# Weight sums of layer two's P pairs: made in the third block and kept for the fourth

## The chip, the cores and the metric

The kernel runs on one core of one Trainium2 chip. The metric is the device time of one launch in microseconds (us). Before the change three runs took 1447.68, 1449.65 and 1452.13 us; the median is 1449.65 us. The profile is of one further execution, which took 1452.83 us.

## The reference, cut to what matters

The model is two layers over 2048 tokens of width 1024. Each layer normalises, scales and shifts its input, multiplies it by `w_in` (1024 x 3072), mixes, gates, and multiplies by `w_out`:

```python
for l in range(DEPTH):                       # 2
    mod = c_act @ w_ada[l] + b_ada[l]
    shift, scale, gate = jnp.split(mod, 3, axis=-1)
    h = rms_norm(x, g_pre[l]) * (1.0 + scale[:, None, :]) + shift[:, None, :]
    proj = h @ w_in[l]                       # u_a, b_a, c_a, gate_a, u_p, gate_p: 512 columns each
    y_a = b_a * causal_depthwise_conv(c_a * u_a, w_conv[l]) * jax.nn.silu(gate_a)
    y_p = causal_multiscale_pool(u_p, w_pool[l], pool_scale[l]) * jax.nn.silu(gate_p)
    y = jnp.concatenate([y_a, y_p], axis=-1) @ w_out[l]
    x = x + gate[:, None, :] * rms_norm(y, g_post[l])
```

All of it is in float32.

## The kernel before, in words

The tokens are cut into two halves of 1024. Layer and half give four blocks: first (0,0), second (0,1), third (1,0), fourth (1,1), in this order. A block is an in-projection, with the mixing behind it, and then an out-projection; the out-projection also prepares the next block's input `h`.

A float32 matmul is made of three: every operand is split into a rounded high part (a cast on ScalarE, ACT in the profile) and a remainder (a subtraction on VectorE, DVE), and high x high, high x remainder and remainder x high are summed. So each weight tile goes through a load, a cast (line 211, or 777) and a subtraction (line 221, or 787) before TensorE (PE) may use it.

There are two forms of in-projection. The plain one (`in_phase`) takes one group of 128 output columns at a time, 8 k steps of 6 matmuls of 128x512. The other (`in_seven`) takes two groups as a pair, with the seven products of a Strassen scheme instead of eight; a product is 12 matmuls. The pairs are called P (`up` with `gp`), A (`ua` with `ca`) and B (`ba` with `ga`), four of each, i = 0 to 3. The seven products need the weight quarters A11, A12 and A22 and the four sums S1 to S4 of quarters. The first block is plain throughout; the second is plain for i = 0 and 1 and in pairs for i = 2 and 3; the third and fourth are in pairs.

Where the sums come from is what the change touches. In the second block's pairs they are made on the spot: four quarters are loaded by SyncE (SP), `add` makes the sums on VectorE (lines 758 to 760 and 765), and casts and remainders follow as for any weight. Layer two's sums are needed twice, in the third block and in the fourth; they are made ahead, as background tasks, with high part and remainder, and stored to a DRAM tensor `sums`, from which GpSimd (POOL) loads them at line 740 straight into their place. The tasks for the A and B pairs run in the first block. Those for the P pairs, `sum_task`, two for each pair, run in the second block's plain part. One of them takes two landing places, four loads (line 456), seven VectorE instructions (lines 464 to 467, 474, 476), three casts and four stores by POOL (lines 478 to 481).

The same plain part has other background tasks. First come 16 fills, which load parts of `h` (line 1123), and 8 mix tasks, which load a weight tile, multiply it on TensorE (line 421) and store it. Then come 16 finish tasks for the first block's output, with the sum tasks between them: a finish task loads two tiles (lines 1180 and 1181), multiplies and adds on VectorE (lines 1184 and 1186), stores the new residual by POOL (line 1191), and adds its square up (lines 1197 and 1200). Fills, mixes, finish and sum tasks all land in one pool `l`, five places of 128x512, and each place is free again when the last reader, a store by POOL in many cases, is done with it.

The order of the work is written out by the program: engines take their instructions in exactly the order in which the code issues them, so an instruction that waits holds up all behind it on its engine or queue. `Paced` spreads the tasks: each of 72 steps (of 96; tasks are taken from step 14 on) gets an equal share of the tasks' written costs, E2 = 0.7 us per VectorE instruction. Weights of the plain part are loaded up to five half groups ahead and their remainders made three ahead, counting the one in work; a half group is 24 matmuls. In the pairs, loads go out 6 products ahead, casts 4 and remainders 3 (`LOAD, HIGH, SETTLE`); the products' weights lie in a ring of seven places.

`working(t, r, l, w, v)` sets the numbers of places: t for wide scratch tiles, r for 128x512 scratch halves, l for landing tiles, w for raw weights, v for a partial sum.

Of the kernel before, what the change touches and what calls it, by code (L numbers as in the profile page):

```python
# [12 lines left out]
P = 128  # L13
# [9 lines left out]
NCG = 4  # L23
# [10 lines left out]
def trunk(ctx: ExitStack, tc: tile.TileContext, xt, c, wada, vec, rcp, win, wupt, wpool, wout, out):  # L34
    nc = tc.nc
# [4 lines left out]
    @contextmanager  # L40
    def working(t, r, n, w, v):

        with ExitStack() as st:
            for name, bufs in (("t", t), ("r", r), ("l", n), ("w", w), ("v", v)):
                if bufs:
                    held[name] = st.enter_context(tc.tile_pool(name=name + str(t), bufs=bufs, reuse_waits="tile"))
            yield
# [38 lines left out]
    for l in range(DEPTH):  # L86
# [10 lines left out]
    sums = {  # L97
        (l, n): dram.tile([P, 2, 4, KH * P], F32R, name=f"sums{l}_{n}") for l in range(DEPTH) for n in range(3 * NCG)
    }
# [9 lines left out]
    class Work:  # L109
# [5 lines left out]
        def __init__(self):  # L115
            self.q = []
# [314 lines left out]
    PAIRS = [(kind, i) for i in range(NCG) for kind in ("P", "A", "B")]  # L431
# [269 lines left out]
    def in_weights(l, order, first, places):  # L701
        return Weights([w_src(l, *order[n], h) for n in range(first, len(order)) for h in range(2)], places)

    PRODUCTS = (
        ("A11", "B11"), ("S2", "T2"), ("S3", "T3"), ("S1", "T1"), ("A12", "B21"), ("A22", "T4"), ("S4", "B22"),
    )
# [3 lines left out]
    SUM = {"S1": 0, "S2": 1, "S3": 2, "S4": 3}  # L710
    LOAD, HIGH, SETTLE = 6, 4, 3

    class Sevenths:


        def __init__(self, l, ring, pairs, made=False):
            self.l, self.ring, self.pairs, self.made = l, ring, pairs, made
            self.ops, self.raws = {}, {}
            self.nm = 7 * len(pairs)
            self.loaded = self.highs = self.settled = 0  # L720
# [11 lines left out]
        def load(self, upto):  # L732
            while self.loaded < min(upto, self.nm):
                m = self.loaded
                n, q = divmod(m, 7)
                a = PRODUCTS[q][0]
                if a in SUM and not self.made:
                    kind, i = self.pairs[n]
                    t = self.place(m)
                    nc.gpsimd.dma_start(t.rearrange("p a b c -> p a (b c)"), sums[self.l, PAIRS.index((kind, i))][:, :, SUM[a]])  # L740
                elif not self.made:
                    self.raws[m] = self.quarter(n, *QUARTER[a])
                elif q == 0:
                    self.raws[m] = self.raws[m + 1] = self.quarter(n, 0, 0)
                    self.raws[m + 2] = self.quarter(n, 1, 0)
                    self.raws[m + 5] = self.quarter(n, 1, 1)
                elif q == 4:
                    self.raws[m] = self.raws[m + 2] = self.quarter(n, 0, 1)
                self.loaded += 1
# [19 lines left out]
        def high(self, upto):  # L769
            self.load(upto)  # L770
            us = 0
            while self.highs < min(upto, self.nm):
                m = self.highs
                if m in self.raws:
                    if self.made:
                        us += self.add(m)
                    nc.scalar.copy(self.place(m)[:, 0], self.raws[m].rearrange("p (a b) -> p a b", b=P))  # L777
                self.highs += 1
            return us

        def low(self, upto):
            us = 0
            while self.settled < min(upto, self.nm):
                m = self.settled
                if m in self.raws:
                    t, raw = self.ops[m], self.raws.pop(m).rearrange("p (a b) -> p a b", b=P)
                    nc.vector.tensor_tensor(t[:, 1], raw, t[:, 0].bitcast(F32), op=ALU.subtract)  # L787
                    us += E2
                self.settled += 1
            return us  # L790

        def settle(self, upto):
            return self.high(upto) + self.low(upto)
# [730 lines left out]

        return ws, closing, done

    with working(5, 6, 5, 6, 2), tc.manual_schedule():
        plain = [(kind, i) for kind, i in IN_ORDER if i < PLAIN]
        pairs = [(kind, i) for kind, i in PAIRS if i >= PLAIN]
        first = in_weights(0, plain, 0, turned(ws.places, 16))  # L1530
        h, fills, opening, hrhs = out_phase(0, 0, y, 0, 1, ws, hplaces, yorder, first, True)
        ring = first.places + hplaces[8 : 8 + KH]
        wts = Sevenths(0, ring, pairs, True)
        later = Later()
        mixes = [mix_task(1, g, n, later) for g in range(NCG) for n in range(2)]
        fins = finish_tasks(0, 0, later)
        sums_ = [sum_task(1, n, u, False) for n, u in mine("P")]
        tasks = between(fills, mixes) + between(fins, sums_)
        in_phase(0, 1, hrhs, tasks, later, None, None, first.places, wts, first, opening, plain)
        hp = {}  # L1540
        for k in range(KH):
            hp["B11", k], hp["B21", k], hp["B22", k] = hplaces[k], hplaces[KH + k], hplaces[12 + k]
        it = iter(yorder)
        for name in ("T2", "T3", "T1", "T4"):
            for k in range(KH):
                hp[name, k] = next(it)
        ws, closing, done = block_end(0, 1, hp, ring, pairs, False, (3, 2, 3, 2, 2, 2))
        kept = in_seven(0, 1, h, [], None, [], later, wts, closing, pairs)
        y, yorder, wplaces, hplaces, _ = done(kept)
    with working(5, 8, 6, 3, 2), tc.manual_schedule():  # L1550
        for n, (l, b) in enumerate(blocks[2:], 2):
            lplaces = yorder[4:]
            ring = wplaces[1:] + yorder[:4] + wplaces[:1]
            wts = Sevenths(l, ring, PAIRS)
            h, fills, opening, _ = out_phase(*blocks[n - 1], y, l, b, ws, hplaces, lplaces, wts)
            hp = {}
            it = iter(hplaces)
            for k in range(KH):
                for name in ("B11", "T1", "T3", "T2"):
                    hp[name, k] = next(it)  # L1560
            it = iter(lplaces)
            for name in LATE:
                for k in range(KH):
                    hp[name, k] = next(it)
            later = Later()
            tasks = finish_tasks(*blocks[n - 1], later)
            if (l, b) == (1, 0):
                tasks = between(tasks, [ada_task(1, 2 * KT + k) for k in range(KT)])
                tasks += [call_task(lambda: ada_fin(1, 2, 0, KT), 0.3)]
            last = n + 1 == len(blocks)  # L1570
            ws, closing, done = block_end(l, b, hp, ring, PAIRS, last, (3, 3, 3, 3, 2, 0))
            kept = in_seven(l, b, h, fills, opening, tasks, later, wts, closing, PAIRS)
            y, yorder, wplaces, hplaces, spare = done(kept)
            if last:
                out_last(l, b, y, ws, spare)
# [41 lines left out]
```

## Time and profile before

| | |
|---|---|
| median of three runs | 1449.65 us |
| profiled execution | 1452.83 us, span 1451.0 us |
| TensorE busy | 1385.0 us, 95% |
| VectorE busy | 984.0 us, 68% |
| ScalarE busy | 523.8 us, 36% |
| GpSimd busy | 227.9 us, 16% |
| DMA | 306.97 MB, mean 212 GB/s |

Busy TensorE time says where it waited, not how fast it was: matmuls are pipelined, and the granted clock stands apart. A wait is put down to what released it. PEld is the load of weights into TensorE, which overlaps the matmuls. In the profile's names `ws` is a weight's place, `raw` a raw weight, `fin` a finish task's tile, `x` the stored residual.

### The profile page before, as it was taken

Reading aid. Unit: us, or ns where it says so; the run is one execution under the profiler, and the core shown is the slowest. Engines: PE = TensorE matmul, PEld = TensorE weight load, DVE = VectorE, ACT = ScalarE, POOL = GpSimd, SP = SyncE. Lnnn points to the kernel's source line nnn. Section 1 sums busy time; section 2 is a strip of 40 time slices with the busy share of each in tenths; the row PEclk is TensorE's granted clock in tenths of the full one; section 3 lists DMA queues with packets and bytes.
Section 4 is the critical chain, followed back from the end, with each engine's and each line's share of the span. In section 5 each row is a group of like instructions: output and inputs, shape, how many; then the busy total and the mean of one; then the engine's idle time right before and its main releaser. Section 6 shows DMA issues by size and latency. Waiting matters only on the chain.

```text
span 1451.0 us, 18013 instructions
## 1 busy us (share of the span) xinstructions
PE 1385.0 (95%) x6178; PEld 1134.8 (78%) x6178; DVE 984.0 (68%) x1645; ACT 523.8 (36%) x905; POOL 227.9 (16%) x365
## 2 busy tenths in 40 slices
PE   8999999999999676999999999999999999999996
PEld 4778887888887465788788888888888888888796
DVE  7765978876656466687776767677775756657555
ACT  5333442244554222322665422212656311112521
POOL 0001222211102222000022222121022111211000
PEclk9999999999999898999999999999999999999998
DMA  8516988865637676322566988687567787877422
GB/s 310 178 44 205 330 279 270 269 228 202 219 114 252 204 242 217 131 73 102 167 210 217 293 272 252 220 278 247 195 232 252 235 253 211 252 240 230 160 91 88
DMA packets 149598, 306.97 MB, mean 212 GB/s; under 512 B 16641, under 2 KB 33025, under 8 KB 149506
## 3 DMA queue, kind: packets, MB, share of 16 engines
q1 hardware_dynamic: 100658, 179.44, 38.0%
q0 software_dynamic: 48848, 126.38, 26.0%
q8 instruction: 48, 0.79, 0.2%
q14 instruction: 44, 0.36, 0.1%
HBM read 225.54 MB, written 80.22 MB: 211 GB/s over the span
## 4 chain that ended last, share of the span: by engine, by line
PE 74%; DVE 8%; issue 8%; DMA 7%; ACT 2%; POOL 1%; SPq 1%; DVEq 0%; POOLq 0%; ACTq 0%
PE ps_in L868 37%; PE ps_out L395 22%; PE ps_in L395 13%; DMA raw<-win 2%; DMA late<-late 1%; DVE ws L221 1%; DMA fin<-xt 1%; DVE y L188 1%; DMA adaw<-wada 1%; DMA raw<-wout 1%; DMA ws<-sums 1%; PE ps_stat L1321 0%; PE ps_warm L1304 0%; DVE win L497 0%; PE ps_wu L421 0%
## 5 line engine op out<-in xcount | busy, mean ns | idle before, releaser
L868 PE MATMUL ps_in<-h,ws 128*128 128x512 f32 x2520 | 572.8, 389 | 0.6 <-DMA ws<-sums 0.6
L868 PEld LDWEIGHTS ps_in<-h,ws 128*128 128x128 f32 x2520 | 472.9, 188 | 99.3 <-DMA ws<-sums 1.0
L395 PE MATMUL ps_in<-h,ws 128*128 128x512 f32 x1392 | 335.9, 402 | 32.3 <-DVE ws L221 28.0
L395 PE MATMUL ps_out<-y,ws 128*128 128x512 f32 (+1 forms) x1728 | 354.6, 366 | 2.9 <-ACT ws L211 1.2
L395 PEld LDWEIGHTS ps_out<-y,ws 128*128 128x128 f32 x1728 | 298.4, 189 | 58.4 <-DVE ws L221 1.9
L395 PEld LDWEIGHTS ps_in<-h,ws 128*128 128x128 f32 x1392 | 269.3, 195 | 92.5 <-DVE ws L221 30.9
L221 DVE TENSOR_TENSOR ws<-raw,ws 128x512 fp32r<-128x512 f32 x122 | 83.3, 687 | 71.0 <-ACT ws L211 71.0
L211 ACT CAST ws<-raw 128x512 fp32r<-128x512 f32 x122 | 74.3, 619 | 121.9 <-PE ps_in L395 44.5
L777 ACT CAST ws<-raw 128x512 fp32r<-128x512 f32 x108 | 64.7, 618 | 122.2 <-PE ps_in L868 45.8
L740 POOL DMA_DIRECT2D ws<-sums x96 | 67.8, 707 | 207.2 <-PE ps_in L868 185.2
L395 PE MATMUL ps_in<-h,w 128*128 128x512 f32 x336 | 81.8, 402 | 5.3 <-DVE h L387 2.8
L395 PEld LDWEIGHTS ps_in<-h,w 128*128 128x128 f32 x336 | 63.5, 191 | 22.7 <-DVE h L387 3.6
L787 DVE TENSOR_TENSOR ws<-raw,ws 128x512 fp32r<-128x512 f32 x108 | 74.0, 685 | 4.7 <-ACT ws L777 4.7
L1067 POOL DMA_DIRECT2D ysp<-yg x48 | 26.2, 546 | 221.4 <-ACT yg L1066 220.6
L1186 DVE TENSOR_TENSOR fin<-fin 128x512 f32<-128x512 f32 x48 | 32.9, 686 | 31.8 <-DMA fin<-xt 31.7
L891 ACT COPY v<-ps_in 128x512 f32<-128x512 f32 x30 | 17.6, 588 | 101.9 <-PE ps_in L868 101.9
L912 ACT ACTIVATE second<-second 128x1024 f32<-128x1024 f32 x20 | 21.2, 1062 | 87.3 <-DVE second L906 84.0
L1197 ACT ACTIVATE fin<-fin 128x512 f32<-128x512 f32 x28 | 17.7, 631 | 92.8 <-DVE fin L1186 63.9
L267 DVE SCALAR_TENSOR_TENSOR adaw<-adaw,cb 128x512 f32<-128x512 f32 x64 | 42.7, 686 | 12.3 <-DMA adaw<-wada 12.3
L906 DVE TENSOR_TENSOR second<-ps_in,v 128x512 f32<-128x512 f32 x20 | 13.8, 690 | 43.2 <-PE ps_in L868 43.2
L1075 DVE TENSOR_TENSOR acc<-acc,sq 128x512 f32<-128x512 f32 x42 | 28.5, 691 | 19.9 <-ACT sq L1072 19.9
L1066 ACT ACTIVATE yg<-ps_out,gg 128x512 f32<-128x512 f32 x48 | 33.1, 689 | 13.8 <-PE ps_out L395 13.7
(191 smaller groups left out, 1345.8 us busy)
## 6 DMA issues: line engine op xcount, KB each, us to landing
ws<-sums POOLq DMA_DIRECT2D x96, 512.0 KB, 7.4
raw<-win SPq DMA_DIRECT2D x122, 256.0 KB, 5.1
adaw<-wada SPq DMA_DIRECT2D x64, 256.0 KB, 5.1
raw<-wout SPq DMA_DIRECT2D x64, 256.0 KB, 4.8
sums<-raw POOLq DMA_DIRECT2D x48, 256.0 KB, 5.7
ysp<-yg POOLq DMA_DIRECT2D x48, 256.0 KB, 3.6
fin<-ysp SPq DMA_DIRECT2D x48, 256.0 KB, 5.3
yraw<-yin SPq DMA_DIRECT2D x42, 256.0 KB, 4.0
```

Source lines behind the costliest of these rows:

```text
L211: nc.scalar.copy(self.ws[m][:, 0], self.raws[m].rearrange("p (a b) -> p a b", b=P))
L221: nc.vector.tensor_tensor(t[:, 1], raw, t[:, 0].bitcast(F32), op=ALU.subtract)
L267: nc.vector.scalar_tensor_tensor(w[n], w[n], 1.0, cb[:, n * HS : (n + 1) * HS], op0=ALU.mult, op1=ALU.mult, accum_out=m[:, l, j : j + 1])
L395: nc.tensor.matmul(ps[s], lhsT=ws[k // KH][:, wi, k % KH, :], rhs=rhs(k, ri, s), start=first and (wi, ri) == PASSES[0], stop=last and (wi, ...
L740: nc.gpsimd.dma_start(t.rearrange("p a b c -> p a (b c)"), sums[self.l, PAIRS.index((kind, i))][:, :, SUM[a]])
L777: nc.scalar.copy(self.place(m)[:, 0], self.raws[m].rearrange("p (a b) -> p a b", b=P))
L787: nc.vector.tensor_tensor(t[:, 1], raw, t[:, 0].bitcast(F32), op=ALU.subtract)
L868: nc.tensor.matmul(ps, lhsT=ops[m][:, wi, k, :], rhs=h[hn][k][:, ri, :], start=p < 4 and k == 0 and (wi, ri) == (0, 0), stop=k == KH - 1 a ...
L1066: nc.scalar.activation(t, ps[s], AF.Copy, scale=gg[:, l, j : j + 1])
L1067: nc.gpsimd.dma_start(ysp[l, b][:, j, s * HS : (s + 1) * HS], t)
L1075: tt(accs[s], accs[s], q, op=ALU.add)
L1186: nc.vector.tensor_tensor(e[1], e[1], e[0], op=ALU.add)
```

## The change

P1, P2 and P3 are listed in `SPOT`. Their six sum tasks leave the second block's plain part; P0's two stay. In the third block the products of these three pairs are made as in the second block's pairs, from four quarters, and `store` (line 801) sends each finished sum, high part and remainder, from its place to `sums` by POOL. The fourth block loads all sums as before. The pools change: in the second block six landing places instead of five and five raw places instead of six; in the third and fourth block seven scratch halves instead of eight, five landing places instead of six, five raw places instead of three.

```diff
+    SPOT = [("P", i) for i in range(1, NCG)]
...
-        def __init__(self, l, ring, pairs, made=False):
-            self.l, self.ring, self.pairs, self.made = l, ring, pairs, made
+        def __init__(self, l, ring, pairs, made, keep=False):
+            self.l, self.ring, self.pairs, self.made = l, ring, pairs, [p in made for p in pairs]
+            self.keep = keep
...
-                if a in SUM and not self.made:
+                if a in SUM and not self.made[n]:
...
-                elif not self.made:
+                elif not self.made[n]:
...
-                    if self.made:
+                    if self.made[m // 7]:
                         us += self.add(m)
...
                     us += E2
+                    self.store(m, t)
                 self.settled += 1
             return us
+
+        def store(self, m, t):
+
+            n, a = m // 7, PRODUCTS[m % 7][0]
+            if self.keep and a in SUM:
+                dst = sums[self.l, PAIRS.index(self.pairs[n])][:, :, SUM[a]]
+                nc.gpsimd.dma_start(dst, t.rearrange("p a b c -> p a (b c)"))
...
-    with working(5, 6, 5, 6, 2), tc.manual_schedule():
+    with working(5, 6, 6, 5, 2), tc.manual_schedule():
...
-        wts = Sevenths(0, ring, pairs, True)
+        wts = Sevenths(0, ring, pairs, pairs)
...
-        sums_ = [sum_task(1, n, u, False) for n, u in mine("P")]
+        sums_ = [sum_task(1, n, u, False) for n, u in mine("P") if PAIRS[n] not in SPOT]
...
-    with working(5, 8, 6, 3, 2), tc.manual_schedule():
+    with working(5, 7, 5, 5, 2), tc.manual_schedule():
...
-            wts = Sevenths(l, ring, PAIRS)
+            wts = Sevenths(l, ring, PAIRS, SPOT if b == 0 else (), b == 0)
```

From line 713 on the lines move by 3 to 11: 740 becomes 743, 758 to 760 become 761 to 763, 787 becomes 790, 1184 and 1186 become 1195 and 1197, 1191 becomes 1202, 1200 becomes 1211.

VectorE in the second block's plain part, before; `raw_4069` and `s_4100` belong to a sum task of P1, `ws` at line 221 is a weight's remainder:

```order
L221 TENSOR_TENSOR ws<-raw,ws 128x512
L1186 TENSOR_TENSOR fin<-fin 128x512
L464 TENSOR_TENSOR s_4100<-raw_4069,raw_4072 128x256
L465 TENSOR_TENSOR s_4100<-raw_4069 128x256
L466 TENSOR_TENSOR raw_4069<-s_4100,raw_4069 128x256
L467 TENSOR_TENSOR raw_4072<-raw_4072,raw_4069 128x256
L1200 TENSOR_TENSOR xacc<-xacc,fin 128x512
L1184 TENSOR_TENSOR fin<-fin,ry 128x512
L1186 TENSOR_TENSOR fin<-fin 128x512
L221 TENSOR_TENSOR ws<-raw,ws 128x512
L609 TENSOR_TENSOR cv<-cv,sga 128x1024
```

The second remainder stands behind two finish additions and four instructions of a sum task, each of which needs its own landed tile. The same place now, ahead of the same gating (line 609):

```order
L221 TENSOR_TENSOR ws<-raw,ws 128x512
L1197 TENSOR_TENSOR fin<-fin 128x512
L1195 TENSOR_TENSOR fin<-fin,ry 128x512
L1197 TENSOR_TENSOR fin<-fin 128x512
L1211 TENSOR_TENSOR xacc<-xacc,fin 128x512
L1195 TENSOR_TENSOR fin<-fin,ry 128x512
L221 TENSOR_TENSOR ws<-raw,ws 128x512
L609 TENSOR_TENSOR cv<-cv,sga 128x1024
```

The sum task's instructions are gone, and between two remainders stand parts of three finish tasks.

VectorE in the third block before P1's first product, before (`second`, `cv` and `v` belong to pair B0, which is in work; `adaw` is another background task):

```order
L787 TENSOR_TENSOR ws<-raw,ws 128x512
L267 SCALAR_TENSOR_TENSOR adaw,mod<-adaw,cb 128x512
L906 TENSOR_TENSOR second<-ps_in,v 128x512
L916 TENSOR_TENSOR cv<-ps_in,cv 128x512
L926 TENSOR_TENSOR v<-ps_in,v 128x512
```

and now:

```order
L790 TENSOR_TENSOR ws<-raw,ws 128x512
L761 TENSOR_TENSOR s_6733<-raw 128x512
L762 TENSOR_TENSOR raw<-raw 128x512
L763 TENSOR_TENSOR raw<-s_6733,raw 128x512
L267 SCALAR_TENSOR_TENSOR adaw,mod<-adaw,cb 128x512
L790 TENSOR_TENSOR ws<-raw,ws 128x512
L917 TENSOR_TENSOR second<-ps_in,v 128x512
L927 TENSOR_TENSOR cv<-ps_in,cv 128x512
L790 TENSOR_TENSOR ws<-raw,ws 128x512
L937 TENSOR_TENSOR v<-ps_in,v 128x512
```

Three additions and two remainders have come between B0's evictions (lines 917, 927 and 937).

POOL's queue in the third block around pairs P1 and A1 (`sums_3` and `sums_4` are their sums), before:

```order
L809 DMA yin_0_100<-cv 128x1024
L740 DMA ws<-sums_3_122 128x2x512
L740 DMA ws<-sums_4_123 128x2x512 x2
L1191 DMA x_1_97<-fin 128x512
L740 DMA ws<-sums_4_123 128x2x512
```

and now:

```order
L801 DMA sums_3_122<-ws 256x1x512 x2
L820 DMA yin_0_100<-cv 128x1024
L801 DMA sums_3_122<-ws 256x1x512
L743 DMA ws<-sums_4_123 128x2x512 x2
L801 DMA sums_3_122<-ws 256x1x512
L1202 DMA x_1_97<-fin 128x512
L743 DMA ws<-sums_4_123 128x2x512
```

P1's loads are gone; its four stores stand later in the queue, the last of them behind two loads of A1's sums.

## Rows read from the trace of the kernel before

**Rows 1.** Busy time by stage: stretch, length, PE, PEld, DVE, ACT, POOL, clock, DMA, GB/s.
```profile
399.00:454.00 55.00, 51.92 (x260) 43.42 (x259) 29.89 (x46) 27.41 (x49) 5.14 (x9) 1.00 0.47 156
454.00:593.00 139.00, 102.86 (x392) 80.72 (x391) 79.64 (x141) 36.07 (x71) 33.71 (x52) 0.86 0.67 228
797.00:1016.00 219.00, 219.00 (x967) 181.24 (x966) 158.49 (x261) 59.45 (x98) 45.99 (x70) 1.00 0.83 260
```

**Rows 2.** TensorE in order of time, second block: start, duration, line, count.
```profile
398.68 13.77 PE L395 MATMUL ps_in<-h,ws 128*128 128x512 f32 x60
...
421.42 1.05 PE L421 MATMUL ps_wu<-wp,wupt 128*128 128x128 f32 x8
422.23 4.36 PE L395 MATMUL ps_in<-h,ws 128*128 128x512 f32 x18
...
592.98 7.19 PE L868 MATMUL ps_in<-h,ws 128*128 128x512 f32 x31
```

**Rows 3.** The chain that ended last, the first out-projection: start, us, what.
```profile
311.81 87.04 PE ps_out L395 x384
```

**Rows 4.** TensorE's waits from 398 to 594: total us, times, longest.
```profile
PE ps_in L395 <- DVE ws L221: 28.0, 6, 7.1
...
PE ps_wu L421 <- DMA wupt<-wupt: 3.1, 2, 1.6
PE ps_stat L313 <- ACT ah L368: 2.8, 1, 2.8
PE ps_stat L313 <- DVE al L370: 1.1, 1, 1.1
```

**Rows 5.** Busy time and clock of ten us behind gaps.
```profile
510.00:520.00 10.00, 3.62 (x10) 2.53 (x9) 6.08 (x13) 3.25 (x7) 1.65 (x3) 0.67 0.67 208
```

**Rows 6.** VectorE by line, 454 to 593: busy us, mean ns, idle before.
```profile
L1186 DVE TENSOR_TENSOR fin<-fin 128x512 f32<-128x512 f32 x16 | 11.1, 692 | 31.8 <-DMA fin<-xt 31.7
...
L474 DVE TENSOR_TENSOR s<-s,s13h 128x512 fp32r<-128x512 f32 x8 | 5.5, 684 | 0.0
L464 DVE TENSOR_TENSOR s<-raw,raw 128x256 f32<-128x256 f32 x8 | 3.4, 425 | 13.9 <-DMA raw<-win 13.9
```

**Rows 7.** SyncE's queue, its waits from 398 to 594.
```profile
SPq L1181 <- DMA x<-fin: 26.8, 7, 6.0
...
SPq L1181 <- DMA sums<-raw: 16.2, 2, 11.1
```

**Rows 8.** SyncE's queue in order of time: first and last task load.
```profile
448.30 0.32 SPq L1180 DMA_DIRECT2D fin<-ysp  x1
...
575.88 0.40 SPq L456 DMA_DIRECT2D raw<-win  x1
```

**Rows 9.** DMA issues from 454 to 593: count, KB, median us to landing.
```profile
x<-fin POOLq DMA_DIRECT2D x16, 256.0 KB, 3.4
...
fin<-xt SPq DMA_DIRECT2D x15, 256.0 KB, 3.8
```

**Rows 10.** Busy time over three pairs, twice, and a pair made on the spot.
```profile
854.00:911.00 57.00, 57.00 (x253) 47.23 (x252) 39.92 (x67) 12.66 (x22) 11.92 (x18) 1.00 0.87 264
969.00:1026.00 57.00, 57.00 (x253) 47.18 (x252) 43.41 (x72) 16.92 (x31) 9.16 (x14) 1.00 0.79 246
669.00:688.00 19.00, 19.00 (x86) 15.73 (x85) 17.72 (x25) 4.87 (x9) 0.53 (x1) 1.00 0.35 124
```

**Rows 11.** DMA issues from 797 to 1016, the third block.
```profile
ws<-sums POOLq DMA_DIRECT2D x45, 512.0 KB, 7.5
...
fin<-xt SPq DMA_DIRECT2D x16, 256.0 KB, 6.3
...
x<-fin POOLq DMA_DIRECT2D x16, 256.0 KB, 6.1
```

**Rows 12.** TensorE in order of time after 593: first and last wait (in brackets).
```profile
717.32 8.17 PE L395 MATMUL ps_out<-y,ws 128*128 128x512 f32 x33 [0.19 <-ACT y L185]
...
1438.92 0.70 PE L1258 MATMUL ps_stat<-sq,onesf 128*128 128x256 f32 x2 [0.47 <-ACT sq L1257]
```

## What I expected before the run

> **What bounds the kernel now.** I read the busy time by stage first, then TensorE's waits in the worst stage, then the chain back to their cause. TensorE is busy in every slice, so its waits matter and nothing else does. [rows 1] shows one stage that breaks the pattern: from 454 to 593 us TensorE is busy 102.86 of 139 us and the mean granted clock is 0.86. In the third block (797 to 1016) it is busy all 219 us at clock 1.00. The bad stage is the second block's plain in-projection, which runs from 398.68 to 592.98 [rows 2]: 194.3 us.
>
> What would it take without waits? It has 12 column groups of 8 k steps of 6 matmuls, 576 in all. In a dense stretch 384 matmuls take 87.04 us [rows 3], 0.2267 us each, so 130.6 us. A mix task's matmuls hold TensorE from 421.42 to 422.23 [rows 2], 0.81 us; eight make 6.5. Eight statistics matmuls are 1.8. The floor is 138.9 us, and 55.4 us are lost. TensorE's five waits there add up to 39.2 us, from 28.0 behind VectorE's weight remainders (line 221) down to 1.1 [rows 4]. The other 16.2 us I put down to the clock: between 510 and 520 it is 0.67, after gaps of up to 7.1 us [rows 4, 5], while the stretch from 399 to 454, with gaps of at most 1.6 us, holds 1.00 [rows 1, 4]. A mean of 0.86 is 28% of the 139 us at the lower of the two levels (1.2 GHz), 39 us; losing 16.2 there means TensorE worked 32 of them.
>
> The Trainium skill, "TensorE: Matmul & The Clock Gate", section "HAM oscillation", says the clock falls in idle gaps and that the price is paid again after each. By that rule the 16.2 us leave with the gaps; were the low clock a property of this stage, they would stay and the sum below would end near 1420. The stretch before 454 speaks for the rule.
>
> Why are the remainders late? Not for lack of VectorE: it is busy 79.64 of 139 us. It stands in its queue before the finish tasks (line 1186, 31.7 us for DMA) and the sum tasks (line 464, 13.9 us for DMA) [rows 6], and the remainders stand behind these. Their loads are late because SyncE stands before landing places: it waits 26.8 us for stores of finish tiles and 16.2 us for stores of sums [rows 7]. So the bound is a ring of five places, each held until its store has landed. From 448.30 to 575.88 [rows 8] the 16 finish and 8 sum tasks draw 48 tiles: 2.66 us per tile, so each place is held 13.3 us.
>
> **The change, part by part.** *Second block.* Six of eight sum tasks go. On VectorE each is six instructions on 256 columns of 0.42 us and one on 512 of 0.68 [rows 6], 3.2 us, in all 19 us, and with them three quarters of the 13.9 us that it waited in them. Going too are 24 loads on SyncE's queue and 24 stores on POOL's, 9.4 MB of the 31.7 MB that 228 GB/s moved in 139 us [rows 1]. The ring then has 36 tiles and six places. How long do they need? At 13.3 us each, 36 x 13.3 / 6 = 80 us. The shortest cycle of a finish tile is its load 3.8, two VectorE operations 1.4 and its store 3.4 [rows 6, 9], 8.6 us, which gives 52 us. How long may they take? By the costs written in the program the tasks hold 55.8 us instead of 74.4 over the same 72 steps, 0.775 per step. Fills and mixes (16.0) take 20.6 steps from step 14, so the finish tasks have steps 35 to 86, 51 steps of 1.36 us: 69 us. The middle of 52 and 80 is 66, so the ring no longer sets the pace. Even 80 would be 11 us late at the end, and remainders are due two half groups of 24 matmuls before their use, 10.9 us. What is late next are the waits that aren't on remainders, 3.1 on a mix tile and 2.8 and 1.1 on the statistics [rows 4]: I leave these 7.0 us and 1 more. Gain: 55.4 - 8 = 47.4 us; its bounds are 55.4 and, by the first rival, 32. The weights' raw places fall from six to five there, but only three loads are ever ahead of their remainder in this stage, so I cost that at nothing; SyncE's other work covers it.
>
> *Third block.* For P1, P2 and P3 VectorE gets 4 additions and 4 remainders more per pair, 24 instructions of 0.68 us [rows 6]: 16.4 us. ScalarE gets 12 casts; it is busy 59.45 of 219 us [rows 1]. SyncE's queue gets one quarter more per pair, and three of the four go out together, six products ahead. POOL's queue swaps 12 loads of 512 KB for 12 stores. Cover for VectorE: from 854 to 911, one pair each of P1, A1 and B1, it is busy 39.92 of 57 us, and 5.5 more makes 80%; from 969 to 1026 43.41, which makes 86% [rows 10]. In the second block, where pairs are already made on the spot, it is busy 17.72 of 19 us, 93%, and TensorE all 19.00 [rows 10]. So I count it as hidden; were the cover gone, all 16.4 us would be on the path.
>
> The added wait is POOL's: each store waits for VectorE's remainder, and behind it in the queue stand the next pair's sums and the finished tiles. A remainder is made three products before its use, a product is 12 matmuls, 2.72 us, so a store has 8.2 us before and 2.7 us during the use until its place may be overwritten. The trace has no such store; the nearest rows are 7.5 us for a 512 KB load in this stage and 6.1 us for a 256 KB store [rows 11]. Both are below 10.9, so no product waits for its place.
>
> *Third and fourth block, places.* Raw tiles go from 3 to 5, landing from 6 to 5, scratch halves from 8 to 7. TensorE's six waits after 593, the first 0.19 at 717.32 and the last 0.47 at 1438.92, sum to 3.9 us [rows 12], so no more is to be won there. In the third block 48 landing tiles pass in 69 steps of 2.72 us, 188 us: five places allow 19.6 us each, and the cycle is 6.3 + 1.4 + 6.1 = 13.8 [rows 6, 11]. For everything after 593 I take 2 us lost, between 3.9 won and 16.4 lost.
>
> *Sum.* 47.4 - 2 = 45.4 us. The profiled execution took 1452.83 us (span 1451.0), which gives 1407.4. It lies 3.2 us above the median of the three runs, 1449.65; for a median I take 45.4 off that: **1404 us**.
>
> **The rivals.** *The ring stays the bound.* The 22.3 MB that remain in the stage at its floor of 88 us (of 139) would be 253 GB/s, about the third block's 260, where a finish load takes 6.3 us and not 3.8 [rows 1, 9, 11]. Then places are held longer and the waits return. It stops itself: at 228 GB/s, today's rate, landing is as now and 22.3 MB take 98 us, 10 more than the floor. With 5 us of lowered clock that is 1419. For it: the page "DMA: Bandwidth & Descriptors" of the Trainium skill, section "Issuing engines are not separate DMA queues", has all queues share 16 engines, and the third block agrees. Against it: 16 of the 18 tasks left are finish tasks, whose stored tile goes out after two VectorE operations.
>
> *VectorE's new work isn't hidden.* If the additions stand before evictions that TensorE waits for, the third block gives back 16.4 us instead of 2: 1418. For it: 86% in the last pairs; against it, the 93% stretch without a gap.
>
> *Slower than before.* The third block's landing ring, cut from six to five, jams as the second block's did. It decides from 19.6 us per tile; to eat the 47 us, 48 tiles must take 235 us, 24.5 us each. If the second block's ratio of held to shortest time (13.3 / 8.6) held for 13.8, it would be 21.3 us, 205 us in all, 17 us lost, still faster. At 25 us it is 240 us, 52 lost: 1456. For it: 512 KB stores now stand on POOL between the stores that free these places. Against it: the tasks here are spread over twice the time per step that they have in the second block.
>
> *No change.* The order of the instructions shows the six tasks gone, so only a floor that I have missed in the stage would do this: 1450.
>
> **How the numbers follow.** Forecast 0.76; ring still the bound 0.13; VectorE not hidden 0.06; slower 0.03; no change 0.02. Low end: all 55.4 us come back and nothing is lost, 1394. High end: 1422, which takes in the first two rivals; both together would be 1433. Differences under about 0.3% (4 us) can't be told from none: faster 0.95, same 0.02, slower 0.03.
>
> **What would show it.** The plain stage, from the last matmul of the first out-projection to the first made product, should take about 147 us instead of 194, at clock 0.97 or more, with VectorE waiting under 10 us in the finish additions (line 1186, now 1197). SyncE's waits on stored sums should all but go. The third block should stay at 219 us busy without gaps, VectorE busy about 175 us in it. It is wrong if the plain stage stays above 165 us, or if TensorE shows more than 5 us of waits between the third block's first and last product.

## The result, and the profile after

Four runs of the changed kernel took 1398.34 to 1401.83 us, median **1399.74 us**; the kernel before, on the same chip, 1449.59. The ratio is 0.9656, with a 95% interval of 0.9637 to 0.9676: 49.9 us faster, where 45.4 had been predicted.

In the profiled executions the difference is 52.9 us (1452.83 and 1399.89). Nearly all of it lies in one stage. First the stages of the kernel after (columns as in [rows 1]: stretch, its length, busy time of PE, PEld, DVE, ACT and POOL, granted clock, DMA share, GB/s); the first three answer to [rows 1] and [rows 5], the last is the third block.

```profile
399.00:454.00 55.00, 53.94 (x269) 45.37 (x268) 31.67 (x49) 29.71 (x52) 6.07 (x11) 1.00 0.57 190
454.00:539.00 85.00, 85.00 (x376) 70.30 (x375) 59.84 (x97) 25.72 (x47) 15.57 (x27) 1.00 0.73 246
510.00:520.00 10.00, 10.00 (x46) 8.29 (x45) 9.41 (x15) 3.48 (x7) 1.08 (x2) 1.00 0.62 208
743.00:962.00 219.00, 217.94 (x960) 179.79 (x959) 173.55 (x286) 66.78 (x111) 44.85 (x69) 1.00 0.83 262
```

The stretch after 454 us, 139 us long in [rows 1], is now 85 us, TensorE busy in all of it, and the clock, 0.67 between 510 and 520 in [rows 5], is 1.00. TensorE's timeline in the kernel after, from the start of the second block's plain part to the first made product; it answers to [rows 2]:

```profile
397.90 2.43 PE L395 MATMUL ps_in<-h,ws 128*128 128x512 f32 x10
...
451.46 1.13 PE L421 MATMUL ps_wu<-wp,wupt 128*128 128x128 f32 x8 [1.06 <-DMA wupt<-wupt]
452.34 42.46 PE L395 MATMUL ps_in<-h,ws 128*128 128x512 f32 x186
...
495.11 35.55 PE L395 MATMUL ps_in<-h,ws 128*128 128x512 f32 x156
...
530.97 8.35 PE L395 MATMUL ps_in<-h,ws 128*128 128x512 f32 x36
539.15 21.02 PE L879 MATMUL ps_in<-h,ws 128*128 128x512 f32 x92
```

The stage runs from 397.90 to 539.15: 141.25 us instead of 194.3, 2.35 above the floor of 138.9. One wait is left of those in [rows 4], 1.06 us on a mix tile. From there to the end it is 858.95 us (1398.1 - 539.15) and was 858.0 (1451.0 - 592.98): all that follows the stage costs 0.95 us more. With 0.78 us won ahead of the stage, 53.05 + 0.78 - 0.95 = 52.9. The 0.78 are chance: four kernels that are the same up to there (this one and three of the runs below) begin the stage between 396.65 and 399.33 us.

What stood in the queues, in the kernel after: VectorE's finish additions and sum tasks (groups by line, 453 to 539 us; after the bar busy time, mean ns of one, and idle time before them with what ended it), SyncE's waits (399 to 540: us in total, times, longest), SyncE's first and last background load, and landings (448 to 541, median us from issue), which answer to [rows 6 to 9].

```profile
L1197 DVE TENSOR_TENSOR fin<-fin 128x512 f32<-128x512 f32 x16 | 11.1, 691 | 5.9 <-DMA fin<-xt 5.5
...
L464 DVE TENSOR_TENSOR s<-raw,raw 128x256 f32<-128x256 f32 x2 | 0.9, 426 | 5.5 <-DMA raw<-win 5.5
```

```profile
SPq L1192 <- DMA x<-fin: 12.7, 4, 7.5
...
SPq L1192 <- DMA sums<-raw: 1.2, 1, 1.2
...
SPq L1191 <- DMA sums<-raw: 0.3, 1, 0.3
```

```profile
447.30 0.33 SPq L1191 DMA_DIRECT2D fin<-ysp  x1
...
520.07 0.42 SPq L456 DMA_DIRECT2D raw<-wu  x1
```

```profile
fin<-xt SPq DMA_DIRECT2D x16, 256.0 KB, 4.9
x<-fin POOLq DMA_DIRECT2D x16, 256.0 KB, 4.9
```

VectorE stands idle 5.9 us before the finish additions, not 31.8, and SyncE hardly at all for stored sums. Its 36 tiles pass in 72.8 us, 2.02 each, so one of six places is held at most 12.1 us. A landing takes longer than in [rows 9], 4.9 us instead of 3.8 and 3.4, at 246 GB/s instead of 228.

### The profile page after: what moved, and what is told of

It reads as the page before. It is cut to its first block, busy times and chain, and to the rows that moved or that the text cites. A ratio compares the mean times of both kernels' runs of the same rounds, so it can differ in the third digit from the quotient of the medians.

```text
span 1398.1 us, 17890 instructions
## 1 busy us (share of the span) xinstructions
PE 1370.5 (98%) x6178; PEld 1127.0 (81%) x6178; DVE 980.9 (70%) x1627; ACT 523.1 (37%) x899; POOL 210.2 (15%) x341
## 4 chain that ended last, share of the span: by engine, by line
PE 83%; DVE 7%; DMA 5%; issue 3%; ACT 2%; SPq 1%; POOL 0%; DVEq 0%; ACTq 0%; POOLq 0%
PE ps_in L879 37%; PE ps_out L395 23%; PE ps_in L395 20%; DMA adaw<-wada 1%; DMA ysp<-yg 1%; PE ps_wu L421 1%; DVE ws L221 1%; DVE y L188 1%; PE ps_warm L1315 1%; PE ps_stat L1332 1%; DMA raw<-wout 1%; DVE adaw L267 0%; DMA sums<-s13h 0%; DMA raw<-win 0%; DMA wupt<-wupt 0%
## 5 line engine op out<-in xcount | busy, mean ns | idle before, releaser
L879 PE MATMUL ps_in<-h,ws 128*128 128x512 f32 x2520 | 572.8, 389 | 0.9 <-DMA ws<-sums 0.9
L879 PEld LDWEIGHTS ps_in<-h,ws 128*128 128x128 f32 x2520 | 473.0, 188 | 99.5 <-DMA ws<-sums 1.3
L395 PE MATMUL ps_in<-h,ws 128*128 128x512 f32 x1392 | 322.1, 392 | 0.0
L395 PEld LDWEIGHTS ps_in<-h,ws 128*128 128x128 f32 x1392 | 261.5, 189 | 54.2
L780 ACT CAST ws<-raw 128x512 fp32r<-128x512 f32 x117 | 70.3, 619 | 180.2 <-DMA raw<-win 71.9
L221 DVE TENSOR_TENSOR ws<-raw,ws 128x512 fp32r<-128x512 f32 x122 | 83.2, 687 | 67.8 <-ACT ws L211 67.4
L211 ACT CAST ws<-raw 128x512 fp32r<-128x512 f32 x122 | 74.5, 620 | 148.0 <-PE ps_in L395 75.6
L743 POOL DMA_DIRECT2D ws<-sums x84 | 59.5, 709 | 176.1 <-PE ps_in L879 158.4
L790 DVE TENSOR_TENSOR ws<-raw,ws 128x512 fp32r<-128x512 f32 x117 | 80.1, 685 | 7.0 <-ACT ws L780 6.8
L267 DVE SCALAR_TENSOR_TENSOR adaw<-adaw,cb 128x512 f32<-128x512 f32 x64 | 42.9, 686 | 16.2 <-DMA adaw<-wada 16.2
L917 DVE TENSOR_TENSOR second<-ps_in,v 128x512 f32<-128x512 f32 x20 | 13.8, 689 | 33.8 <-PE ps_in L879 33.7
L1195 DVE TENSOR_TENSOR fin<-fin,ry 128x512 f32<-128x512 f32 x48 | 32.9, 685 | 3.1 <-DMA fin<-ysp 3.1
```

The source lines that it names most:

```text
L211: nc.scalar.copy(self.ws[m][:, 0], self.raws[m].rearrange("p (a b) -> p a b", b=P))
L267: nc.vector.scalar_tensor_tensor(w[n], w[n], 1.0, cb[:, n * HS : (n + 1) * HS], op0=ALU.mult, op1=ALU.mult, accum_out=m[:, l, j : j + 1])
L395: nc.tensor.matmul(ps[s], lhsT=ws[k // KH][:, wi, k % KH, :], rhs=rhs(k, ri, s), start=first and (wi, ri) == PASSES[0], stop=last and (wi, ...
L879: nc.tensor.matmul(ps, lhsT=ops[m][:, wi, k, :], rhs=h[hn][k][:, ri, :], start=p < 4 and k == 0 and (wi, ri) == (0, 0), stop=k == KH - 1 a ...
L1195: nc.vector.tensor_tensor(e[0], e[0], ry[l, b, s], op=ALU.mult)
```

## The experiments

In all runs the kernel before ran beside on the same chip, at 1450.8 to 1453.5 us. A "plain stage" is read from TensorE's timeline as above; "clock and rest" is the stage less 138.9 less TensorE's waits in it; "of it clock" is what the granted clock explains of that (TensorE's busy time x (1 - granted clock), added up over pieces of 1 us, an estimate); "ring" is the time from SyncE's first to its last background load, "held" the same x places / tiles, the time that a tile has a place if no place ever stands empty.

| run | tiles, places | plain stage | waits | clock and rest | of it clock | ring | held | median | ratio, 95% |
|---|---|---|---|---|---|---|---|---|---|
| before | 48, 5 | 194.3 | 39.2 | 16.2 | 12.5 | 128.0 | 13.3 | | |
| places only | 48, 6 | 174.8 | 22.7 | 13.2 | 10.5 | 106.4 | 13.3 | 1433.65 | 0.9889 (0.9870-0.9908) |
| seven places | 48, 7 | 161.8 | 13.1 | 9.8 | 7.6 | 99.3 | 14.5 | 1419.41 | 0.9791 (0.9772-0.9809) |
| tasks only | 36, 5 | 147.7 | 4.7 | 4.1 | 1.7 | 79.4 | 11.0 | 1408.76 | 0.9714 (0.9693-0.9735) |
| after | 36, 6 | 141.3 | 1.1 | 1.3 | 0.0 | 72.8 | 12.1 | 1399.74 | 0.9656 (0.9637-0.9676) |
| DMA back | 48, 6 | 167.8 | 19.3 | 9.6 | 6.1 | 103.2 | 12.9 | 1427.52 | 0.9832 (0.9804-0.9859) |
| VectorE's work back | 36, 6 | 150.8 | 7.1 | 4.8 | 1.6 | 81.2 | 13.5 | 1408.37 | 0.9698 (0.9670-0.9727) |

**The tasks, or the place?** My theory was a ring: tiles x hold / places sets the pace. The rival: the sum tasks' own work. Two runs have one half of the second block's change each, and a third goes one place further. Every landing place more is a raw place less; raw places were not changed by themselves.

```diff
 # tasks only: the changed kernel
-    with working(5, 6, 6, 5, 2)
+    with working(5, 6, 5, 6, 2)
 # places only: the kernel before
-    with working(5, 6, 5, 6, 2)
+    with working(5, 6, 6, 5, 2)
 # seven places: the kernel before
-    with working(5, 6, 5, 6, 2)
+    with working(5, 6, 7, 4, 2)
```

> The changed kernel with the second block's places put back: five landing places, six raw ones. Six sum tasks are gone, 36 tiles pass. Ring theory: lateness of the tasks = tiles x hold / places - time available - the 10.9 us that remainders are ahead. With the hold of before, 13.3 us: 36 x 13.3 / 5 - 69 - 10.9 = 16 us of waits, and with the clock lost as before (16.2 for 39.2 of waits) 23 us: plain stage about 162 us, time about 1421. If the places are held shorter because the stores of the sums are gone, down to the 11.2 us that the changed kernel's landings make (4.9 load, 1.4 VectorE, 4.9 store): 81 us, no wait, 1400. Rival (the sum tasks' own work on VectorE and the DMA was the cost, places are beside the point): within 2 us of the changed kernel, 1400, with the hold still 13 us or more.

> The kernel before with six landing places and five raw ones in the second block, and nothing else: 48 tiles pass. Ring theory: 48 x 13.3 / 6 = 106 us, less 77 available (56.5 steps of 1.36 us at before's pace) and 10.9: 18 us of waits instead of 39, with clock 26 instead of 55: plain stage about 165 us, time about 1420. Rival (sum tasks' own work): no more than 5 us gained, 1445 to 1450. In both the clock should follow the waits: about 0.4 us lost for each us of wait.

> The kernel before with seven landing places and four raw ones in the second block, all eight sum tasks kept. Ring theory: 48 x 13.3 / 7 = 91 us, less 77 and 10.9: 3 us of waits and 1 of clock on top of the waits that are not on remainders: plain stage 145 to 150 us, time about 1404, if four raw places do not hold up the made pairs behind it (their stretch of 114.4 us is read apart). Rival (sum tasks' own work): 1445 to 1450.

Without the six tasks 42.0 us of the 49.9 are won; with the sixth place alone 17.1, and with a seventh 31.4. Places matter, so the rival in its pure form falls. But the ring gave the pace and not the waits. Without the tasks, and with five places, a tile is held 11.0 us, near the 11.2 of the case that had no wait and 1400 us; yet 8.8 us over the floor were lost, and 1408.76 lies between the two cases. With six places 106 us were reckoned and 106.4 came; yet 35.9 us over the floor were lost, not 26. With seven, 99.3 us came, not 91, and 22.9 us were lost, not 10. What keeps TensorE waiting is seen in the run with six places only: VectorE's timeline (start, length, instruction, idle time before and what ended it), and then TensorE's.

```profile
499.29 0.42 DVE L464 TENSOR_TENSOR s<-raw,raw 128x256 f32<-128x256 f32 x1 [6.56 <-DMA raw<-win]
499.64 0.42 DVE L465 TENSOR_TENSOR s<-raw 128x256 f32<-128x256 f32 x1
500.09 0.42 DVE L466 TENSOR_TENSOR raw<-s,raw 128x256 f32<-128x256 f32 x1
500.55 0.42 DVE L467 TENSOR_TENSOR raw<-raw,raw 128x256 f32<-128x256 f32 x1
500.89 0.68 DVE L221 TENSOR_TENSOR ws<-raw,ws 128x512 fp32r<-128x512 f32 x1
```

```profile
501.63 3.78 PE L395 MATMUL ps_in<-h,ws 128*128 128x512 f32 x8 [5.79 <-DVE ws L221]
```

A sum task needs both its tiles before its first instruction; VectorE stands 6.56 us for them, and the remainder that TensorE waits 5.79 us for is four instructions behind. The loads were late because SyncE had stood 6.3 us for a place that a finish task's addition on VectorE (line 1200) freed, and 2.1 us for one that a stored sum freed. Here a single late task was enough; the mean pace doesn't show it.

**What of a sum task costs?** Two runs put one half of the six tasks back into the changed kernel.

```diff
 # VectorE's work back
-        sums_ = [sum_task(1, n, u, False) for n, u in mine("P") if PAIRS[n] not in SPOT]
+        sums_ = [
+            sum_task(1, n, u, False) if PAIRS[n] not in SPOT else vector_task(1, n, u) for n, u in mine("P")
+        ]
 # vector_task: no load, no store; six instructions on 256 columns and one on 512, on data held on the chip
 # DMA back
-        sums_ = [sum_task(1, n, u, False) for n, u in mine("P") if PAIRS[n] not in SPOT]
+        sums_ = [sum_task(1, n, u, False) for n, u in mine("P")]
 # sum_task of P1 to P3: loads, casts and stores, without the seven VectorE instructions
```

> The changed kernel with six tasks put back into the second block that do only what a sum task does on VectorE: six instructions on 256 columns, one on 512, on data that lies there already, with the same written cost; no place, no load, no store. Ring theory: VectorE is busy 60.8 of the 86 us from 453 to 539 and takes 19.2 us more into its gaps: 0 to 5 us lost, 1400 to 1405. Rival (VectorE's share of the sum tasks was what TensorE waited for): 19 us or more come back, 1419 to 1427 with the clock.

> The changed kernel with the six sum tasks put back, but without their VectorE instructions: two landing places, four loads, three casts, four stores each (what they store is overwritten in the third block). 48 tiles through six places. The kernel before with six places needed 106 us for its 48 tiles and lost 33.5 us against the changed kernel; without seven VectorE instructions a sum tile is held some 3 us less, 16 of 48 tiles, so about 100 us for the ring. Ring theory: most of the loss comes back, plain stage 160 to 172 us, time 1419 to 1431. Rival (VectorE's share): 1400 to 1405.

The stage grows by 9.6 us with VectorE's share and by 26.6 with places and DMA; both together, in the run with six places only, by 33.5. So the larger part, some three quarters of the two, lies with the places, loads, casts and stores, as expected; what of it is the places and what the traffic was not parted. VectorE's 9.6 are more than my 0 to 5 and half of the rival's 19. VectorE and TensorE at the largest gap of that run:

```profile
471.56 0.42 DVE L464 TENSOR_TENSOR s<-raw,raw 128x256 f32<-128x256 f32 x1 [5.28 <-DMA raw<-win]
...
474.36 0.68 DVE L221 TENSOR_TENSOR ws<-raw,ws 128x512 fp32r<-128x512 f32 x1
```

```profile
475.09 12.73 PE L395 MATMUL ps_in<-h,ws 128*128 128x512 f32 x48 [2.82 <-DVE ws L221]
```

VectorE stood 5.28 us for a load of one of the two real sum tasks left, and the remainder was behind it. The changed kernel stands 5.5 us ahead of the same two tasks and TensorE does not wait. But the two runs differ in the order too: the tasks are dealt out evenly between the finish tasks, so with eight of them P0's two come earlier (first load at 447.86 us instead of 478.47). The 9.6 us are the instructions and that order together; what the instructions alone cost is not shown.

**The third block's work.** Is it hidden, and how far does the cover reach?

```diff
 # sums left out
-            wts = Sevenths(l, ring, PAIRS, SPOT if b == 0 else (), b == 0)
+            wts = Sevenths(l, ring, PAIRS, ())
-... sums[self.l, PAIRS.index((kind, i))]
+... sums[self.l, PAIRS.index((kind, 0 if kind == "P" else i))]
-    with working(5, 7, 5, 5, 2)
+    with working(5, 8, 6, 3, 2)
 # all on the spot
-    SPOT = [("P", i) for i in range(1, NCG)]
+    SPOT = list(PAIRS)
-            made = [sum_task(1, n, u, True) for n, u in mine("AB")]
+            made = []
-        sums_ = [sum_task(1, n, u, False) for n, u in mine("P") if PAIRS[n] not in SPOT]
+        sums_ = []
```

> The changed kernel without its work in the third block: the six sum tasks are gone and nothing takes their place, P1 to P3 load the sums of P0 (this part of the computation is left out); pools of the third and fourth block as before. Theory (additions, casts and stores of the third block are hidden): within 2 us of the changed kernel, 1397 to 1400; the stretch from the first made product of the second block to the end 858 us as before. Rival (VectorE's 16.4 us are partly on the path and something else was won): 1385 to 1395.

> All twelve pairs' sums made on the spot in the third block and stored there; no sum task is left in the first and second block. VectorE in the third block: 173.6 us of 219 now, and nine more pairs of 5.5 us make 223. Theory (the work was hidden because VectorE had gaps, and the cover ends at 100%): the third block is longer by 4 us at least and by 10 to 25 with jams, against 2 to 4 won in the first block and the plain stage: 1403 to 1425, waits of TensorE on VectorE in the third block. Rival (VectorE's queue there is not what TensorE would wait for): 1395 to 1398.

Sums left out: 1397.74 us (0.9643, 0.9624-0.9663), 2.0 below the changed kernel with overlapping intervals, and 858.06 us from the first made product to the end, as before (858.0). So the work costs 0.9 us in the profiled executions; the medians can't tell it from nothing. All on the spot: 1408.19 us (0.9700, 0.9668-0.9731). The third block from its first product to the out-projection is 243.8 us instead of 232.1, while 5.8 us are won up to the second block's first made product (533.38 against 539.15). One row of that block by stage, and waits in it, TensorE's and ScalarE's:

```profile
735.00:979.00 244.00, 234.23 (x1020) 190.12 (x1018) 220.77 (x366) 87.16 (x152) 45.09 (x71) 1.00 0.82 259
```

```profile
PE ps_out L395 <- ACT ws L211: 4.3, 1, 4.3
PE ps_in L879 <- ACT ws L780: 3.7, 6, 1.5
```

```profile
ACT ws L780 <- DVE raw L763: 44.3, 9, 6.8
```

VectorE is busy 220.77 of 244 us, 90%. TensorE waits six times, 3.7 us, for casts at line 780, where ScalarE in turn stands for the additions of `add` (line 763). The longest wait, 4.3 us at the start of the out-projection, is another: it is for a cast of an out-projection weight, and that cast stood for its load (ScalarE):

```profile
978.76 0.62 ACT L211 CAST ws<-raw 128x512 fp32r<-128x512 f32 x1 [5.64 <-DMA raw<-wout]
```

SyncE issued such loads only from 972.95 on, behind others that had stood up to 13.4 us for tiles which VectorE (line 188) had still to use. So the cover is not used up by P1 to P3 but is by all twelve. The busy share alone does not say so: in [rows 10] 93% went without a wait. Nor is VectorE shown to be the only cause, for this run adds loads and casts as well.

**The third block's places.** Rival 3 said that a ring of five could jam there.

```diff
 # four places, six places: the changed kernel
-    with working(5, 7, 5, 5, 2)
+    with working(5, 7, 4, 6, 2)
+    with working(5, 7, 6, 4, 2)
 # weights on their own queue: with four places
-            nc.sync.dma_start(...)
+            queue = nc.scalar if self.l else nc.sync
+            queue.dma_start(...)
```

> The changed kernel with four landing places in the third and fourth block instead of five (raw places six). My ring reckoning: 48 tiles in 188 us allow 15.7 us each, the shortest cycle is 13.8 us, so nothing is lost: 1399 to 1403, no wait of TensorE in the third block. Rival (a place there is held as in the second block, 1.55 times the shortest cycle, 21.3 us): 48 x 21.3 / 4 = 256 us, 68 too many, less what remainders are ahead: 1450 or more.

> The changed kernel with the sixth landing place of the third and fourth block back (raw places four instead of five). With four landing places 12 us were lost, where my reckoning by the mean pace of the ring said none. Theory (with five the weight loads behind a wait for a place on SyncE's queue are still in time; TensorE shows no wait in the third block): 1397 to 1401, no difference. Rival (the loss goes on with a smaller step): 2 to 4 us won, 1395 to 1398.

Four places: 1411.79 us (0.9721, 0.9695-0.9746), 12 us lost where I had reckoned none, or 9.4 by the two ratios, which allow for the chips. Six: 1401.08 (0.9645, 0.9615-0.9675), no difference. So five is the smallest of the three numbers that is enough. Where do the 12 us arise with four? In the profiled executions 11.1 lie behind the plain stage, 8.1 of them in the third block's in-projection (240.2 us against 232.1), where TensorE's waits grow from 0.9 to 5.6 us. The longest of them, by SyncE, ScalarE and TensorE:

```profile
874.92 0.43 SPq L1191 DMA_DIRECT2D fin<-ysp  x1
880.83 0.33 SPq L1192 DMA_DIRECT2D fin<-xt  x1
881.20 1.39 SPq L732 DMA_DIRECT2D raw<-win  x2
```

```profile
882.67 0.62 ACT L780 CAST ws<-raw 128x512 fp32r<-128x512 f32 x1 [10.07 <-DMA raw<-win]
```

```profile
883.35 70.09 PE L879 MATMUL ps_in<-h,ws 128*128 128x512 f32 x300 [1.82 <-ACT ws L780]
```

SyncE stood for a finish tile's place until 880.83, 5.4 us of it until VectorE had used an `adaw` tile; the weight quarters behind were issued at 881.20, the cast came at 882.67 and TensorE at 883.35. Behind this gap the granted clock is 0.50 from 884.4 to 886.4 us, and the slower work costs some 1.7 us more. It looked like SyncE's order; that was tested.

> The run with four landing places in the third and fourth block, with the weight quarters of these two blocks issued from ScalarE's queue instead of SyncE's, where they stand behind loads of the background tasks that wait for a place. Theory (the 12 us are lost in SyncE's order: a wait for a place holds up the weights behind it): most comes back, 1399 to 1405, and the casts' waits for raw weights in the third block (78.6 us with SyncE's queue) fall below 40. Rival (the ring of four itself is too slow, the tasks run late and VectorE's order passes that on): 1409 to 1414.

It took 1415.00 us (0.9732, 0.9708-0.9756): the theory falls. The casts' wait for raw weights did drop, from 78.6 to 27.1 us, below 40 as it demanded, but the time did not; 1415.00 and 1411.79 can't be told apart, as the ratios show. The Trainium skill ("DMA: Bandwidth & Descriptors", "Issuing engines are not separate DMA queues") has it that DMAs begun by several engines interleave on the same DMA engines, and that another issuing engine saves only the issuing. The time agrees, since it did not fall; the 51.5 us less in the casts' wait are more than issuing, for the loads no longer stood behind a wait for a place. What grew instead is ScalarE's wait for the additions of `add`, from 14.2 to 31.7 us, and VectorE's wait for the other background tasks' tiles, the first row with four places on SyncE's queue, the second with the weights on their own:

```profile
DVE adaw L267 <- DMA adaw<-wada: 16.4, 3, 6.5
```

```profile
DVE adaw L267 <- DMA adaw<-wada: 24.3, 6, 7.6
```

With five places that was 3.0 us. So the ring itself is late, and VectorE's order hands it on: that is argued from these rows. They point at the `adaw` tiles: SyncE's waits for a landing place of a finish tile that end when VectorE has used an `adaw` tile sum to 24.3 us with four places and to 11.1 with five. No run gave these tiles places of their own, and what it costs that ScalarE's queue now holds loads among its casts was not measured.

**Versions that go on from there.** P0 on the spot as well; and, since the second block's tasks are now few, its plain part cut to i = 0, so that i = 1 too runs in pairs, with ten finish tasks and the mix tasks among them.

```diff
 # all P
-    SPOT = [("P", i) for i in range(1, NCG)]
+    SPOT = [("P", i) for i in range(NCG)]
 # plain for i = 0 alone, on top of it
-PLAIN = 2
+PLAIN = 1
-        tasks = between(fills, mixes) + between(fins, sums_)
+        tasks = between(fills, fins[:6])
-        kept = in_seven(0, 1, h, [], None, [], later, wts, closing, pairs)
+        kept = in_seven(0, 1, h, [], None, between(fins[6:], mixes), later, wts, closing, pairs)
```

> The changed kernel with P0 made on the spot as well: the last two sum tasks leave the second block, 32 tiles of finish tasks remain. Theory (the plain stage is at its floor of 138.9 but for 2.3 us, and the third block hides 5.5 us more of VectorE's work): plain stage 139 to 141 us, time 1396 to 1400, too close to the changed kernel to be told apart for certain. Rival (P0 is the third block's first pair, its raw quarters come when the block opens and its loads collide with the fills): TensorE waits 2 to 5 us at the third block's start, 1400 to 1404.

> As the run with all P pairs on the spot, and the second block plain for i = 0 alone: six groups of 288 matmuls (65.3 us) become three pairs of 252 (57.1 us), 8.2 us less for TensorE. Six finish tasks stay in the plain part, ten and the mix tasks go into the pairs. Theory (the tasks of this block leave VectorE room now that the sums are gone): 1389 to 1395. Rival (VectorE's cover ends: nine made pairs of 15 us and ten finish tasks of 2.1 are 156 us and more of some 171, in lumps): waits of TensorE on VectorE in the pairs, 1400 to 1415.

All P: 1400.42 us (0.9643, 0.9613-0.9672); the plain stage is 139.95 us without a wait of TensorE, yet the whole can't be told from the changed kernel. Plain for i = 0 alone: **1393.58 us** (0.9607, 0.9572-0.9641), below both kernels; against all P, on the same chip, 6.8 us, though the two intervals overlap. The second block's in-projection takes 246.94 us (397.06 to 644.00) instead of 254.19, so 7.25 of the 8.2 reckoned come. Its two parts, by stage:

```profile
398.00:463.00 65.00, 65.00 (x288) 53.64 (x287) 45.62 (x71) 30.24 (x52) 4.86 (x9) 1.00 0.56 186
463.00:644.00 181.00, 180.43 (x827) 150.09 (x826) 152.51 (x230) 63.35 (x113) 12.93 (x24) 1.00 0.45 152
```

VectorE is busy 152.51 of 181 us in the second part, 84%, and TensorE does not wait for it.

## Why the prediction was right, and what was mis-sized

- **The bound.** Right. The 55.4 us were waits, most of them for remainders behind background tasks, and what goes with waits, most of it the clock. All P has no wait in the stage and takes 139.95 us: the floor of 138.9 holds to 1 us.
- **What is left.** Mis-sized: 8 us were kept back, 2.35 came, 5.65 of the 7.5 us by which the profiled difference exceeds 45.4 (of the others, 1.05 are the 2 us taken for the rest of the kernel less 0.95, and 0.78 are the chance ahead of the stage). I had taken the waits on the statistics (2.8 and 1.1 in [rows 4]) as a thing of their own; they are gone, as in all P, so they were lateness passed on. Of the mix tiles' 3.1 us 1.1 stayed. The fifth wait in the 39.2 us, on a cast, is not on a remainder either, and was counted as won without a word; it did go (TensorE, 398 to 594, before):

```profile
PE ps_in L395 <- ACT ws L211: 4.2, 1, 4.2
```

- **The clock.** Right in the main: of the 16.2 us all but 1.3 left with the gaps, and the granted clock no longer falls in the stage. But not all of it was the clock: before, the granted clock explains 12.5 us (TensorE worked 25 us at the lower level, not the 32 reckoned). About 1 us stays without any wait, as all P shows, and what the remaining 2 to 3 us were is open. In the seven rows of the table the clock's part goes to nothing with the waits, from 12.5 us at 39.2 to 0.0 at 1.1, but not in proportion: 13.1 us of waits lost 7.6, 19.3 lost 6.1. The Trainium skill ("TensorE: Matmul & The Clock Gate", "HAM oscillation") has the price paid again after each gap; the fall to nothing agrees with it.
- **The ring.** The 72.8 us measured lie within the 52 to 80 reckoned, but the program's own pace was reckoned at 69 us, so they do not show how fast the ring alone would be. The step from pace to TensorE's waits was not shown by that, and by itself it is too kind to places: it gives the sixth place too much (places only: 35.9 us lost, 26 reckoned) and, with a hold of 13.3 us, the sum tasks too little (tasks only: 8.8 us lost, 23 reckoned). Here both were changed and the two errors don't show in the sum: in that the number was lucky.
- **First rival, the ring stays the bound.** Landings did become longer, 4.9 us, between the 3.8 of before and its 6.3; places were held at most 12.1 us. With 36 tiles and six places that is still enough.
- **Second rival, VectorE's work not hidden.** Wrong for P1 to P3: 173.55 us busy in the third block, about 175 predicted. TensorE's one wait there is 0.91 us, for loaded sums at the block's start. 2 us were taken for everything after 593 and 0.95 came; the third block's in-projection by itself is 1.58 us longer (232.08 and 230.50), and the out-projection ahead of it 1.51 shorter. In the orders ahead of the prediction the three additions stand before B0's three evictions, and only one remainder stands between them. All twelve pairs made on the spot cost 11.7 us there, so the mechanism exists, though not as the only cause.
- **The stores on POOL.** They land in 5.8 us in the third block (twelve, 512 KB), below the 6.1 to 7.5 of [rows 11], and TensorE waits for none of them:

```profile
ws<-sums POOLq DMA_DIRECT2D x32, 512.0 KB, 7.2
...
sums<-ws POOLq DMA_DIRECT2D x12, 512.0 KB, 5.8
```

- **Third rival, the third block's ring.** It did not come, but its margin was reckoned too wide. By the shortest cycle of 13.8 us five places (19.6 us allowed) had much to spare and four (15.7) still enough; four lose 9 to 12 us. So tiles are held longer than the shortest cycle; that a late tile is then handed on by VectorE's order is argued, not shown by a run.

## What to carry to other kernels

Where background tasks share an engine's order with the work that feeds TensorE, look for the instruction that stands for a load, and count what is queued behind it; mean pace and mean busy time don't show it. Taking the task away was worth more here (42.0 us) than another place (17.1 us), and the two do not add up. A ring whose mean reckoning left an eighth to spare (13.8 of 15.7 us) was already too small here; and once a stage runs at its floor, look whether its room now allows the cheaper form of the work.

## What the runs showed of the hardware that I had not expected

Fewer bytes did not make the transfers shorter: with 10 MB less from 448 us to the stage's end (33.24 and 22.90 MB) a finish load of 256 KB took 4.9 us instead of 3.8, while the whole moved at 246 GB/s instead of 229; that the higher rate is the reason was not tried. And the clock's price does not follow the sum of the waits: with seven places 13.1 us of waits came with 7.6 us lost to the lower clock, with the DMA back 19.3 us came with 6.1.
